# A hybrid attention and retention step on one core: an operand refilled block by block by a job, loads and trips moved, constant products in the opening

## The chip, the cores and the metric

The kernel runs on one core of a Trainium2 chip. A core has five engines that work from queues of their own: TensorE (PE in the profile; its weight loads are shown as PEld), VectorE (DVE), ScalarE (ACT), GpSimd (POOL) and SyncE (SP). SP does no arithmetic here; it issues transfers, and so do ACT and POOL beside their work. The metric is the time of one execution on the device in microseconds. A forecast counts as "the same" within 0.3%.

## The reference

One layer of a streaming encoder. Its input is normalised (RMSNorm) and multiplied by one matrix of 2048 x 8192, in eight parts of 8 heads x 128: queries, keys, values and gates of a stick-breaking attention (sb) and of a retention (ret). Cut to what the change touches:

```python
def stick_breaking_block(q, k, v, q_start):
    z = einsum('bqhd,bkhd->bhqk', q, k) * HEAD_DIM ** -0.5
    log_keep = where(strict, log_sigmoid(-z), 0.0)
    later = cumsum(log_keep, axis=3, reverse=True) - log_keep
    a = where(strict, exp(log_sigmoid(z) + later), 0.0)
    return einsum('bhqk,bkhd->bqhd', a, v)

def retention_chunk(q, k, v, s, log_gamma):
    scores = einsum('bihd,bjhd->bhij', q, k) * intra          # intra: decay gamma^|i-j|
    o = einsum('bhij,bjhe->bihe', scores, v) + einsum('bihd,bhde->bihe', q, s) * decay_read
    s_new = s * gamma^n + einsum('bjhd,hj,bjhe->bhde', k, decay_write, v)
    return o, s_new
```

Every branch's output is normalised per head and multiplied by SiLU of its gate; both go through one output matrix of 2048 x 2048, a second RMSNorm and a residual sum. This is done for a prompt of 1024 frames (retention from a zero state) and for 8 running streams of 16 frames each, which have 1024 cached keys and values per head and a retention state per head (`state_ret`). All is float32.

## The kernel before

**Tiles and groups.** The 1024 prompt frames are tiles 0 to 7 of 128 frames, the 8 x 16 sample frames are tile 8 (SAMPLE). Two groups go through the projections one after the other: group 0 holds tiles 0 to 3 and the sample tile, group 1 tiles 4 to 7. The normalised input of a group lies in on-chip memory as the operand `mov`: 16 blocks of 128 features (KT), each split into a high part `mh` and a low part `ml`, four blocks to a tile (WQ). Group 1's normalised input waits in the scratch tensor `s_h` until group 0 has been projected.

**Products.** Each float32 product of a projection is made of three: high x high, high x low and low x high. `split` (L129, L130) makes the parts: ACT writes the high one, DVE the difference. Weights come in blocks `wr` of 256 KB by SP (`load_w`, L213), are split into `wh` and `wl`, and `products` (L227) uses them. `project_rows` (L286) does the same with tokens as rows (`wrn`, `accn`). Weight tiles have four buffers; the tag `mr`, through which blocks of an operand are loaded, has two.

**The opening.** `load_x` brings a tile of x, `mean_square` and `stats` make its scale, `turn` (L370, L372) turns it with 16 products against a diagonal matrix (`dg`) or the identity into `p0t`, which `split` writes into `mov`. The first projection's products are put between the tiles. `stage_rest` prepares group 1's input and stores it in `s_h`.

**Jobs and ticks.** All the work of the heads other than projections is written as generators. A `Job` is stepped by `tick()`, which `products` and `project_rows` call: a tick is one step of a projection (two products in group 0, one in group 1), and at most one job is stepped in a tick. `yield n` waits n ticks. `drain(job)` ticks until a job is done, without products in between. The constants D_... hold those waits, mostly as a pair for group 0 and group 1. `tied(ins)` tells the scheduler, in group 0 alone, to place an instruction no earlier than the product issued last. Within these bounds a scheduler sets the order on each engine; each engine then works its queue in order.

**Retention.** `ret_branch` sends the rotated keys out to memory and reads them back transposed by 32 x 32 squares (`turn_out` by ACT, then `turn_in`, four loads `ro<-s_rk` by SP, then a transposition on DVE): the key trip, D_TO and D_TI ticks long. Then `retention` (L745) loads the head's decay tile `dT` (L747, by SP) and makes four rounds, one per tile: `rs` = keys x queries (L752), `sc` = rs x dT on DVE (L754), `pa` = values x sc (L770) and state x queries (L775), `pS` = keys x values (L785), the new state `S` on DVE. `sample_retention` then loads four pairs of states `st` (L806, by SP), waits, and does the same for the streams (L810 to L836). The head's result makes such a trip too (`Out.finish`: `s_o`, then `ro` or `so`, `do`).

**Attention.** `attention()` of a head projects the queries (`col(0, h)`), drains the attention jobs of the head before, and starts `decode` (the sample streams against the cache: `kc`, `kcT`, `zc`, `vc`, `pd`), then projects the keys (`col(1, h)`) and starts `sb_branch`. In `stick_breaking`, each step makes the scores `z` of one tile, the sigmoids `kp` and `be`, a running product on DVE and the weights; these go to memory by POOL's queue (`turn_out`), come back (`turn_in`) and are transposed on DVE (L576) before the product with the values (`pa`, L616). D_TB ticks lie between the weights and their way out.

**From group 0 to group 1.** With group 0's last head, the gates of both branches are projected together (`project_pair`), weight block by weight block, so that a quarter of `mov` comes free after each pair of blocks. `load_moving` (L205) fills it with group 1's operand: four blocks are drawn ahead of each of the last three pairs, and the last four in the first `project_rows` of group 1.

```python
for k in range(KT):
    r = pool.tile([P, n], F32, name="mr", tag="mr", bufs=bufs)
    nc.sync.dma_start(r, src(k))
    split(hi[q][:, j, at : at + n], lo[q][:, j, at : at + n], r)
    yield D_MR
```

**The end.** `out_panel` and `out_project` multiply by the output matrix, panel by panel; `gpost` is loaded when the heads' memory is free.

Of the kernel before, what the change touches and what calls it, by code (L numbers as in the profile page):

```python
# [58 lines left out]
def tile_hybrid_step(  # L59
# [240 lines left out]
    with ExitStack() as s1:  # L300
# [47 lines left out]
        with tc.tile_pool(name="p0", bufs=2) as p0, tc.tile_pool(name="p0s", bufs=1) as p0s, tc.tile_pool(  # L348
# [16 lines left out]
            def turn(q, xt, scale=None):  # L365
# [34 lines left out]
            for i, t in enumerate(tiles):  # L400
                if i + 1 < len(tiles):
                    scales.append(stats(i + 1))
                cs = slice(i * P, (i + 1) * P)
                for q in range(KT // 4):
                    pt = turn(q, loaded[i], scales[i])
                    split(mov[0][q][:, :, cs], mov[1][q][:, :, cs], pt)
                if i == 1:
                    w4 = list(load_w(col(4, 0)))
                    loaded += [load_x(t) for t in tiles[3:]]
                    acc = acc_banks(g0)  # L410
                    for w in w4:
                        products(mov, acc[:1], g0["pieces"][:1], *w)
# [147 lines left out]
        def stick_breaking(g, h, out, q2, k2, rest):  # L560
# [3 lines left out]
            for step in range(len(todo) + lag):  # L564
# [179 lines left out]

        def retention(gi, g, h, out, rq, rk, rkn, rv):  # L745
            dT = op.tile([P, 2, P], F32, name="dT", tag="dT", bufs=1)
            tied(nc.sync.dma_start(dT, c_dt[:, h]))  # L747

            def scores(i, kind):
# [11 lines left out]
            sc = scores(0, 0)  # L761
            yield D_RET[phase[0]]
            for i in range(4):
                nxt = None
                if i < 3:
# [31 lines left out]
            if SAMPLE in g["tiles"]:  # L797
                yield from sample_retention(h, out, sc, rq, rkn, rv)

        def sample_retention(h, out, sc, rq, rkn, rv):  # L800
            i = 4

            sts = []
            for c in range(4):
                st = ip.tile([P, 2, P], F32, name="st", tag="st", bufs=4)
                tied(nc.sync.dma_start(st, state_ret[0, 2 * c : 2 * c + 2, h].rearrange("b d e -> d b e")))  # L806
                sts.append(st)
            yield 2 * D_RET[phase[0]]
            po = acc_tile()
# [29 lines left out]
        def ret_branch(gi, g, h, rq, rk, rv, rest):  # L839
# [9 lines left out]
            tied(nc.vector.transpose(rkn.rearrange("p k d -> p (k d)")[:, : nt * P], raw))  # L849
# [3 lines left out]
            nc.vector.tensor_scalar(rkn[:, :4, :], rkn[:, :4, :], dec[:, h, 1:2], None, ALU.mult)  # L853
            yield from retention(gi, g, h, out, rq, rk, rkn, rv)
            while "rg" not in rest:
# [33 lines left out]

        from_h = lambda k: s_h[:, k, :]  # L890
        from_y = lambda k: s_y[0][k][:, : 3 * P]
        ret_job = sb_job = sub = loads = after = None
        for gi, g in enumerate(GROUPS):
# [7 lines left out]
            for h in range(H):  # L901
# [70 lines left out]
                def gates():  # L972
# [235 lines left out]
```

## Time and profile before

| | |
|---|---|
| median of 3 runs | 2404.76 us (2398.75 to 2406.34) |
| the profiled execution | 2400.08 us, span 2398.4 us |
| granted TensorE clock, mean | 0.994 |
| PE busy | 2331.4 us, 97% of the span |
| DVE, ACT, POOL busy | 1257.5, 919.6, 643.0 us |
| moved by DMA | 418.68 MB, mean 175 GB/s |

Times are in microseconds from the span's start. A row of the timeline gives start, length, engine, line, operation, output <- inputs and, in brackets, how long the engine stood idle before it and what ended that. A row of the waits gives the engine and line that waited, what for, the sum, the number and the longest. "x32" counts records; a float32 product of 128 x 128 leaves two. A name stands for all buffers of a tile. PEclk is the share of the clock that TensorE was granted.

Group 0's heads run from about 100 to 1120 us, group 1's to about 1985, the output panels to the end.

### The profile page before, as it was taken

Reading aid. Unit: us, or ns where it says so; the run is one execution under the profiler, and the core shown is the slowest. Engines: PE = TensorE matmul, PEld = TensorE weight load, DVE = VectorE, ACT = ScalarE, POOL = GpSimd, SP = SyncE. Lnnn points to the kernel's source line nnn. Section 1 sums busy time; section 2 is a strip of 40 time slices with the busy share of each in tenths; the row PEclk is TensorE's granted clock in tenths of the full one; section 3 lists DMA queues with packets and bytes.
Section 4 is the critical chain, followed back from the end, with each engine's and each line's share of the span. In section 5 each row is a group of like instructions: output and inputs, shape, how many; then the busy total and the mean of one; then the engine's idle time right before and its main releaser. Section 6 shows DMA issues by size and latency. Waiting matters only on the chain.

```text
span 2398.4 us, 40493 instructions
## 1 busy us (share of the span) xinstructions
PE 2331.4 (97%) x14832; PEld 2093.7 (87%) x14832; DVE 1257.5 (52%) x2434; ACT 919.6 (38%) x1933; POOL 643.0 (27%) x1029
## 2 busy tenths in 40 slices
PE   7999999999999999998999999999999999999998
PEld 7998899999999999988878889889898887878787
DVE  7245545445554555445545554554554665564544
ACT  6323333333333333324433434343343454543343
POOL 3144353444344353443202112020221230000000
PEclk9999999999999999999999999999999999999999
DMA  7658879797889879798975565565565666765554
GB/s 244 164 131 209 162 169 196 169 203 166 184 179 194 184 167 194 176 198 198 200 191 151 139 157 149 133 157 146 142 160 139 157 177 181 231 207 176 191 182 132
DMA packets 674890, 418.68 MB, mean 175 GB/s; under 512 B 224513, under 2 KB 619777, under 8 KB 672257
## 3 DMA queue, kind: packets, MB, share of 16 engines
q1 hardware_dynamic: 524272, 285.99, 47.8%
q0 software_dynamic: 32256, 71.36, 13.6%
q10 hardware_dynamic: 118160, 58.74, 9.1%
q8 instruction: 116, 1.90, 0.4%
q14 instruction: 86, 0.70, 0.1%
HBM read 336.24 MB, written 79.69 MB: 173 GB/s over the span
## 4 chain that ended last, share of the span: by engine, by line
PE 87%; DVE 4%; DMA 4%; issue 2%; ACT 1%; POOL 1%; ACTq 0%; DVEq 0%; SPq 0%; POOLq 0%
PE acc L227 45%; PE accn L286 17%; PE a L1029 5%; PE a L1030 5%; PE a L1028 5%; PE pa L616 3%; PE z L586 2%; DMA wr<-w_in 1%; PE zc L659 1%; PE pd L726 1%; DMA mr<-s_h 1%; DVE wl L130 1%; PE pa L770 1%; DVE out L1090 1%; PE rs L752 1%
## 5 line engine op out<-in xcount | busy, mean ns | idle before, releaser
L227 PE MATMUL acc<-mh,wh 128*128 128x256 f32 (+2 forms) x2304 | 664.3, 341 | 6.4 <-ACT wh L129 6.0
L227 PE MATMUL acc<-ml,wh 128*128 128x384 f32 (+2 forms) x2304 | 663.0, 340 | 0.0
L130 DVE TENSOR_TENSOR wl<-wr,wh 128x512 fp32r<-128x512 f32 (+1 forms) x576 | 392.7, 688 | 515.5 <-ACT wh L129 508.3
L227 PE MATMUL acc<-mh,wl 128*128 128x256 f32 (+2 forms) x2304 | 658.9, 339 | 0.6 <-DVE wl L130 0.5
L129 ACT ACTIVATE wh<-wr 128x512 fp32r<-128x512 f32 (+1 forms) x576 | 356.9, 624 | 713.1 <-PE acc L227 243.4
L227 PEld LDWEIGHTS acc<-mh,wh 128*128 128x128 f32 x2304 | 420.2, 189 | 43.3 <-ACT wh L129 7.1
L227 PEld LDWEIGHTS acc<-mh,wl 128*128 128x128 f32 x2304 | 424.4, 189 | 31.4 <-issue 2.1
L227 PEld LDWEIGHTS acc<-ml,wh 128*128 128x128 f32 x2304 | 422.6, 189 | 33.2 <-issue 5.3
L643 POOL DMA_DIRECT2D kc<-cache_sb_k x512 | 332.4, 655 | 369.8 <-DVE kcT L681 207.5
L286 PE MATMUL accn<-whn,mh 128*128 128x256 f32 x1152 | 329.0, 287 | 0.9 <-ACT whn L129 0.8
L286 PE MATMUL accn<-wln,mh 128*128 128x256 f32 x1152 | 326.2, 283 | 0.7 <-DVE wln L130 0.7
L286 PE MATMUL accn<-whn,ml 128*128 128x256 f32 x1152 | 326.0, 283 | 0.0
L286 PEld LDWEIGHTS accn<-whn,mh 128*128 128x128 f32 x1152 | 220.5, 192 | 10.8 <-issue 6.7
L1029 PE MATMUL a<-wl,mh 128*128 128x512 f32 (+1 forms) x576 | 219.7, 381 | 7.8 <-DVE wl L130 7.8
L286 PEld LDWEIGHTS accn<-wln,mh 128*128 128x128 f32 x1152 | 221.2, 192 | 1.7 <-DVE wln L130 0.9
L286 PEld LDWEIGHTS accn<-whn,ml 128*128 128x128 f32 x1152 | 221.2, 192 | 0.0
L1030 PE MATMUL a<-wh,ml 128*128 128x512 f32 (+1 forms) x576 | 218.9, 380 | 0.0
L1028 PE MATMUL a<-wh,mh 128*128 128x512 f32 (+1 forms) x576 | 218.0, 380 | 0.0
L130 DVE TENSOR_TENSOR wln<-wrn,whn 128x512 fp32r<-128x512 f32 x128 | 87.5, 687 | 119.2 <-ACT whn L129 118.5
L129 ACT ACTIVATE whn<-wrn 128x512 fp32r<-128x512 f32 x128 | 80.1, 633 | 152.2 <-PE accn L286 69.8
L1029 PEld LDWEIGHTS a<-wl,mh 128*128 128x128 f32 x576 | 108.3, 188 | 30.5 <-DVE wl L130 9.9
L479 POOL DMA_DIRECT2D be<-s_be x128 | 94.2, 742 | 132.7 <-DMA s_be<-be 114.7
(189 smaller groups left out, 2604.8 us busy)
## 6 DMA issues: line engine op xcount, KB each, us to landing
wr<-w_in SPq DMA_DIRECT2D x384, 256.0 KB, 4.2
wr<-w_out SPq DMA_DIRECT2D x184, 256.0 KB, 3.6
wrn<-w_in SPq DMA_DIRECT2D x128, 256.0 KB, 3.1
kc<-cache_sb_k POOLq DMA_DIRECT2D x512, 64.0 KB, 4.5
vc<-cache_sb_v SPq DMA_DIRECT2D x64, 512.0 KB, 8.6
xt<-x_prompt SPq DMA_DIRECT2D x8, 1024.0 KB, 5.6
xr<-x_prompt SPq DMA_DIRECT2D x8, 1024.0 KB, 6.2
out<-out ACTq DMA_DIRECT2D x12, 512.0 KB, 2.9
```

Of the source, the lines that this page charges most:

```text
L129: nc.scalar.activation(hi, src, AF.Copy)
L130: nc.vector.tensor_tensor(lo, src, hi.bitcast(F32), ALU.subtract)
L227: last = nc.tensor.matmul(a[:, :m], lhs[:, j, :], rhs[w][:, j, o : o + m], start=(w == 0 and j == 0 and n == 0), stop=(w == KT // WQ - 1 a ...
L286: anchor[0] = nc.tensor.matmul(a, lhs[q][:, jj, ts], rhs[:, j, :], start=(w == 0 and j == 0 and n == 0 and t % 2 == 0), stop=(w == KT // 2 ...
L479: q.dma_start(raw[32 * i : 32 * i + 32, :].rearrange("p (k a) -> p k a", a=32), s[:, :, 32 * i : 32 * i + 32].rearrange("k (j b) a -> b (k ...
L586: nc.tensor.matmul(z[:, :c], q2[a][:, i * P : (i + 1) * P], k2[b][:, s : s + c], start=(m == 0), stop=(m == 2),)
L616: nc.tensor.matmul(po[:, :P], at[:, j, :], vn[:, j, :], start=(j == 0), stop=(j == t))
L643: nc.gpsimd.dma_start(kc[32 * i : 32 * i + 32, :].rearrange("p (k d) -> p k d", d=32), cache_k[0, 2 * c + j, s * 512 : (s + 1) * 512, h, 3 ...
L659: mm = nc.tensor.matmul(z[r, :], qp[:, j, r], ready[2 * j + c // 2][:, c % 2, :], start=(j == 0), stop=(j == 1),)
L1028: nc.tensor.matmul(a[:, :width], hi[q][:, j, ts], wh, start=(k == 0), stop=False)
L1029: nc.tensor.matmul(a[:, :width], hi[q][:, j, ts], wl, start=False, stop=False)
L1030: nc.tensor.matmul(a[:, :width], lo[q][:, j, ts], wh, start=False, stop=(k == KT - 1))
```

## The change

1. In the opening, 32 products of a constant tile with itself (`busy`) are put before the first tile and 16 behind it. Their results are not read.
2. `dT` is loaded before the key trip's way back instead of after it, and the key trip has times of its own: D_RO = (32, 44) and D_RI = (32, 34) in place of (32, 23) and (32, 13).
3. The four `st` loads are issued at the third retention round instead of after the last, and the wait of 2 x D_RET ticks behind them goes.
4. D_TB of group 1 is 33 ticks instead of 24, and 22 in heads 4 to 6.
5. Group 1's operand is filled by a job of its own, `refill`: two blocks are loaded ahead; then every D_RF = 6 ticks one block is split and the next but one is loaded; loads and ACT's half of the split are tied to the products. Group 0 no longer draws from `load_moving`; group 1 does as before.

```diff
-D_TB = (17, 24)
+D_TB = (17, 33)
+D_TBL = 22
+WARM = (32, 16)
+D_RF = 6
+D_RO = (32, 44)
+D_RI = (32, 34)
...
+            busy = p0s.tile([P, P], F32, name="busy")
+            nc.vector.memset(busy, 1.37)
+
+            def busy_products(n):
+                pt = p0p.tile([P, 4, P], F32, name="p0t", tag="p0t")
+                for j in range(n):
+                    nc.tensor.matmul(pt[:, j % 4, :], busy, busy, start=True, stop=True)
+
             loaded = [load_x(tiles[0])]
+            busy_products(WARM[0])
...
+                if i == 0:
+                    busy_products(WARM[1])
...
-                        yield D_TB[phase[0]]
+                        yield D_TBL if H - 5 < h < H - 1 else D_TB[phase[0]]
...
-        def retention(gi, g, h, out, rq, rk, rkn, rv):
-            dT = op.tile([P, 2, P], F32, name="dT", tag="dT", bufs=1)
-            tied(nc.sync.dma_start(dT, c_dt[:, h]))
+        def retention(gi, g, h, out, rq, rk, rkn, rv, dT):
...
             for i in range(4):
+                if i == 2 and SAMPLE in g["tiles"]:
+                    for c in range(4):
+                        st = ip.tile([P, 2, P], F32, name="st", tag="st", bufs=4)
+                        tied(nc.sync.dma_start(st, state_ret[0, 2 * c : 2 * c + 2, h].rearrange("b d e -> d b e")))
+                        sts.append(st)
...
-            sts = []
-            for c in range(4):
-                st = ip.tile([P, 2, P], F32, name="st", tag="st", bufs=4)
-                tied(nc.sync.dma_start(st, state_ret[0, 2 * c : 2 * c + 2, h].rearrange("b d e -> d b e")))
-                sts.append(st)
-            yield 2 * D_RET[phase[0]]
...
-            yield D_TO[phase[0]]
+            dT = op.tile([P, 2, P], F32, name="dT", tag="dT", bufs=1)
+            tied(nc.sync.dma_start(dT, c_dt[:, h]))
+            yield D_RO[phase[0]]
             turn_in(s, raw, nc.sync)
-            yield D_TI[phase[0]]
+            yield D_RI[phase[0]]
...
+        def refill(mov):
+            hi, lo = mov
+            blocks = []
+
+            def load(k):
+                blocks.append(wp.tile([P, NB_TOK], F32, name="mr", tag="mr", bufs=2))
+                tied(nc.sync.dma_start(blocks[k], s_h[:, k, :]))
+
+            yield 2 * 3 * WQ - 2 * D_RF
+            load(0)
+            yield D_RF
+            load(1)
+            yield D_RF
+            for k in range(KT):
+                q, j = divmod(k, WQ)
...
+                tied(nc.scalar.activation(hi[q][:, j, :NB_TOK], blocks[k], AF.Copy))
+                nc.vector.tensor_tensor(
+                    lo[q][:, j, :NB_TOK], blocks[k], hi[q][:, j, :NB_TOK].bitcast(F32), ALU.subtract
+                )
+                if k + 2 < KT:
+                    load(k + 2)
+                yield D_RF
...
-                    loads = load_moving(after, 0, *((NB_TOK, from_h), (3 * P, from_y, (ip, 6)))[gi])
+                    if gi == 0:
+                        filling = Job(refill(after))
+                    else:
+                        loads = load_moving(after, 0, 3 * P, from_y, (ip, 6))
```

More of the change, by code (lines that the diff above doesn't have):

```diff
@@ L762, in retention @@
             yield D_RET[phase[0]]
+            sts = []
             for i in range(4):
+                if i == 2 and SAMPLE in g["tiles"]:
[3 more added lines that the diff above has]
+                        sts.append(st)
                 nxt = None
@@ L797, in retention, with sample_retention @@
             if SAMPLE in g["tiles"]:
-                yield from sample_retention(h, out, sc, rq, rkn, rv)
-        def sample_retention(h, out, sc, rq, rkn, rv):
+                yield from sample_retention(h, out, sc, rq, rkn, rv, sts)
+        def sample_retention(h, out, sc, rq, rkn, rv, sts):
             i = 4
-            sts = []
-            for c in range(4):
-                st = ip.tile([P, 2, P], F32, name="st", tag="st", bufs=4)
-                tied(nc.sync.dma_start(st, state_ret[0, 2 * c : 2 * c + 2, h].rearrange("b d e -> d b e")))
-                sts.append(st)
-            yield 2 * D_RET[phase[0]]
             po = acc_tile()
@@ L853, in ret_branch @@
             nc.vector.tensor_scalar(rkn[:, :4, :], rkn[:, :4, :], dec[:, h, 1:2], None, ALU.mult)
-            yield from retention(gi, g, h, out, rq, rk, rkn, rv)
+            yield from retention(gi, g, h, out, rq, rk, rkn, rv, dT)
             while "rg" not in rest:
```

3 lines of the change are left out of this document (added).

## The prediction

> **What bounds the kernel now.** I read the page's busy shares and chain first, then the stretches of 60 us, then every idle time of PE in its timeline.
>
> ```profile
> PE 2331.4 (97%) x14832; PEld 2093.7 (87%) x14832; DVE 1257.5 (52%) x2434; ACT 919.6 (38%) x1933; POOL 643.0 (27%) x1029
> PE 87%; DVE 4%; DMA 4%; issue 2%; ACT 1%; POOL 1%; ACTq 0%; DVEq 0%; SPq 0%; POOLq 0%
> ```
>
> TensorE is busy for 97% and carries 87% of the chain. The change takes no product of the reference away, so all it can win is PE's idle time, 2398.4 - 2331.4 = 67.0 us, and time at a lowered clock. Both sit in few places (columns: stretch, length, busy time of PE, PEld, DVE, ACT, POOL, granted clock, DMA share, GB/s):
>
> ```profile
> 0.00:60.00 60.00, 44.30 (x298) 43.20 (x299) 46.07 (x117) 38.81 (x64) 19.18 (x30) 0.97 0.74 244
> 240.00:300.00 60.00, 55.79 (x407) 52.65 (x406) 30.53 (x75) 19.16 (x45) 20.02 (x31) 0.94 0.82 163
> 1080.00:1140.00 60.00, 53.55 (x366) 48.36 (x364) 34.98 (x86) 27.07 (x62) 21.78 (x37) 0.97 0.80 196
> 1200.00:1260.00 60.00, 54.30 (x382) 47.03 (x381) 26.86 (x61) 21.09 (x46) 4.22 (x7) 0.94 0.71 192
> ```
>
> These four hold 15.7 + 4.2 + 6.5 + 5.7 us of idle PE. PE's timeline names the idle times in brackets, with what ended them:
>
> ```profile
> 10.63 6.71 PE L372 MATMUL p0t<-dg,xt 128*128 128x128 f32 x32 [10.63 <-DVE dg L389]
> 19.52 5.44 PE L372 MATMUL p0t<-dg,xt 128*128 128x128 f32 x32 [2.19 <-DVE p0v L137]
> 30.55 3.73 PE L372 MATMUL p0t<-dg,xt 128*128 128x128 f32 x32
> 270.88 0.80 PE L770 MATMUL pa<-rv,sc 128*128 128x128 f32 x2 [4.21 <-DVE sc L754]
> 541.77 0.49 PE L770 MATMUL pa<-rv,sc 128*128 128x128 f32 x2 [0.43 <-DVE sc L754]
> 543.68 0.56 PE L227 MATMUL acc<-mh,wl 128*128 128x256 f32 x2 [0.16 <-DVE wl L130]
> 1079.37 0.49 PE L770 MATMUL pa<-rv,sc 128*128 128x128 f32 x2 [0.43 <-DVE sc L754]
> 1114.06 0.90 PE L813 MATMUL pa<-st,rq 128*32 128x256 f32 x4 [2.33 <-DMA st<-state_ret]
> 1127.10 0.71 PE L830 MATMUL pSs<-rv,rkn 32*128 32x128 f32 x6 [2.27 <-DVE st L833]
> 1215.01 0.79 PE L227 MATMUL acc<-mh,wh 128*128 128x512 f32 x1 [5.40 <-ACT wh L129]
> 1298.28 1.83 PE L616 MATMUL pa<-vn,kp 128*128 128x128 f32 x14 [1.06 <-DVE kp L576]
> 1398.15 1.16 PE L616 MATMUL pa<-vn,kp 128*128 128x128 f32 x8 [0.66 <-DVE kp L576]
> ```
>
> An idle time also costs clock. Finer stretches:
>
> ```profile
> 20.50:23.50 3.00, 3.00 (x16) 3.00 (x16) 2.03 (x5) 1.81 (x4) 3.00 (x5) 0.50 1.00 384
> 30.00:40.00 10.00, 8.10 (x70) 7.74 (x69) 9.96 (x22) 6.87 (x14) 4.21 (x6) 1.00 0.58 182
> 266.70:276.00 9.30, 5.12 (x20) 4.84 (x21) 7.70 (x21) 3.59 (x9) 4.96 (x9) 0.64 1.09 217
> 1111.60:1124.00 12.40, 9.62 (x53) 7.27 (x52) 6.19 (x13) 4.21 (x10) 8.35 (x14) 0.86 1.05 238
> 1124.00:1147.00 23.00, 18.30 (x127) 15.42 (x126) 16.15 (x34) 12.29 (x23) 9.58 (x17) 0.93 0.71 178
> 1209.00:1219.00 10.00, 4.60 (x18) 3.69 (x17) 3.26 (x8) 2.92 (x8) 0.00 (x0) 0.66 0.84 226
> ```
>
> **The change, part by part.**
>
> *Opening (WARM).* 48 products of a constant are added: 32 (64 passes; the trace counts two for such a product) before tile 0, 16 (32 passes) between tiles 0 and 1. Nothing reads them. The rows at 10.63 and 30.55 show one tile at 6.71 and at 3.73 us, 0.21 and 0.117 us a pass; tile 1 takes 5.44. The cold price is 2.98 + 1.71 = 4.7 us, and 2.19 us of idle time lies between.
>
> ```profile
> 0.97 0.27 DVE L464 MEMSET par<- 128x256 f32 x1
> ```
>
> The constant's memset stands where this row is, so the products start near 1.2 us. Tile 0 took all its 6.7 us to come to speed, tile 1 some 3.5 (to 23.5). With 3.1 to 6.1 us at 0.23 us a pass, the 64 passes end at 10.4 to 11.8 us: against 10.63 nothing to 1.2 us late. Tile 0 then ends at 14.1 to 15.5 instead of 17.34, the second set at 17.9 to 19.3, tile 1 at 21.6 to 23.0 instead of 24.96: 1.9 to 3.3 us earlier. How much reaches the end of the opening is unknown: DVE is busy for 9.96 of the 10 us from 30 on, and only its earlier idle time can be won. Bounds: 1.2 us lost, 4.7 + 2.19 = 6.9 won. I take -2.5, near the middle of what tile 1 wins.
> The Trainium skill ("TensorE: Matmul & The Clock Gate", section on the HAM clock gate) says that the clock is released after about 3.4 us of sustained products, in a window that runs free. The 0.50 between 20.5 and 23.5 agrees. By its figure the first set would end at 1.2 + 3.4 + 49 x 0.117 = 10.3 us, and the sum would hold 0.3 us more gain, an estimate.
>
> *Decay tile and sample states in group 0.* The load of dT moves from after the key trip to before it; the four st loads move 36 ticks ahead of their first product instead of 18, and the 18 ticks of waiting go. Five issues per head are moved, past the ro trip (dT) or two retention rounds (st).
>
> ```profile
> 266.82 0.84 DVE L849 STREAM_TRANSPOSE rkn<-ro 128x640 f32<-128x640 f32 x1 [10.76 <-issue]
> 266.69 14.28 SPq L213 DMA_DIRECT2D wr<-w_in  x9
> 1109.31 1.96 SPq L806 DMA_DIRECT2D st<-state_ret  x4
> ```
>
> Head 1 (stall at 270.88): DVE stood still for 10.76 us until the key rows came, and the next weights were issued only at 266.69, so the wait for weights stays; but products of the retention, no longer behind dT, now fill it. Idle 4.2 us plus (1 - 0.64) x 9.3 = 3.3 us of clock, some 7 us in all, is the most that can go; nothing is the least. About ten products of 0.234 us (two passes at 0.117) done inside the wait save 2.3 us and part of the clock: -3.5.
>
> *The price of that.* In the built order of the changed kernel, heads 2 to 6 of group 0 have 22 products in a row (5 rs, 5 pa, 4 pS, 8 pd) between the query and the key projection of the attention, head 7 has 18, with no projection product among them. Before, dT stood behind them on SP's queue and the scheduler spread them over the next projection. The weights show why: before, one or two blocks of the key projection were loaded ahead of the so trip; now its first block is issued behind that trip. And on ACT its split stands behind the run's own squares and a table load.
>
> ```profile
> 531.86 17.20 SPq L213 DMA_DIRECT2D wr<-w_in  x9
> 536.02 0.38 PE L752 MATMUL rs<-rq,rk 128*128 128x128 f32 x2
> 537.71 0.63 ACT L129 ACTIVATE wh<-wr 128x512 fp32r<-128x512 f32 x1 [9.15 <-DMA wr<-w_in]
> 539.49 1.07 PE L726 MATMUL pd<-vc,kp 128*32 128x256 f32 x16
> 541.46 0.25 DVE L754 TENSOR_TENSOR sc<-rs,dT 128x128 f32<-128x128 f32 x1
> 543.23 1.14 ACT L129 ACTIVATE wh<-wr 128x512 fp32r<-128x512 f32 x2
> 544.56 0.62 ACT L129 ACTIVATE wh<-wr 128x512 fp32r<-128x512 f32 x1
> 545.19 1.28 ACT L138 ACT_TABLE_LOAD   x1
> ```
>
> PE's part of the run is 14 x 0.234 + 1.07 = 4.35 us. ACT: here the table load ends at 546.47, 4.7 us after the first pa; without the three splits ahead of it (1.8 us) 2.9, and with two rounds instead of one about 4.3 (an estimate: a round is six of these short steps of 0.2 to 0.3 us); a first pa comes 0.8 us into the run (rs, then sc at 0.25), the split takes 0.63 and a root 0.2 more: the first key product starts some 6.0 us into the run. PE idles 6.0 - 4.35 = 1.6 us, six times: +9.7. The stalls of 0.43 + 0.16 at 541.77 and 543.68, the first of three such heads (the last at 1079.37), go: -1.8. Together +8. The run begins where the first rs stands here, 536.02. A weight block issued at 531.86, 4.2 us ahead, landed by 537.71, 1.7 us into it: not the limit. Bounds per head: nothing (then -1.8 in all) and the 7 us of the stall at 270.88 (+42).
>
> *refill.* For the 16 blocks of group 1's operand, a job loads one block, splits it and loads the next but one, every 6 ticks; ACT's half is tied to the products. Before, four were drawn at a time, and ACT and SP queued behind them:
>
> ```profile
> ACT mh L129 <- DMA mr<-s_h: 17.5, 10, 5.0
> mr<-s_h SPq DMA_DIRECT2D x14, 256.0 KB, 4.1
> ```
>
> From 1111.6 to 1147 PE idles 2.78 + 4.70 = 7.5 us and loses (1 - 0.86) x 12.4 + (1 - 0.93) x 23 = 3.3 us of clock: 10.8 in all. The st wait (2.33 + 0.44) goes with its earlier load, and its clock loss of 1.7. What remains is bounded by the same two buffers: 4.1 us to land and two splits of 0.7 give 2.75 us a block, 44 us for 16, against 45 us in which they were split before; so ACT will still stand and wait, with weights behind it. I take half of the rest: -4.5 - 3 = -7.5, bounds -10.8 and 0.
> The Trainium skill (same page, "Architectural detail") calls the queues of ScalarE and VectorE strict FIFO, which speaks against tying a split to the products: wh waits behind an mh whose block is late. The 17.5 us above show it; were nothing won beyond the st wait, the sum would hold 3 us less.
>
> *Group 1's times.* D_TB goes from 24 to 33 ticks (22 in heads 4 to 6), the key trip from 23 + 13 to 44 + 34.
>
> ```profile
> PE pa L616 <- DVE kp L576: 5.0, 6, 1.1
> 1805.55 17.27 PE acc L227 x76
> ```
>
> A tick of group 1 is one product, 17.27 / 76 = 0.227 us; nine are 2 us, more than any of these six waits. Four fall in heads 0 to 3, twice 1.06 and 0.66 as at 1298.28 and 1398.15, 3.4 us in all, and go; two in heads 4 and 5 grow by 2 ticks, 0.45 us each. -2.5; bounds -5.0 (all go) and +2 (0.25 us a head, should the later key trip be felt). The retention job grows by 42 ticks and ends some 5 us later, while the first output panel runs; gpost is issued about 20 products later, and DVE's take as well, so the stall behind it keeps its size.
>
> *The wait at 1215.01* keeps its cause (weights behind two trips in the same order): 0, bounds -3 and +3.
>
> Sum: -2.5 - 3.5 + 8 - 7.5 - 2.5 = -8.0 us. The profiled execution took 2400.08 us (span 2398.4 and 1.7 around it), which gives 2392; the median of the runs is 4.7 us above it, 2404.76, and on that I forecast 2396.8, 0.33% less.
>
> **The rivals.**
> *The runs starve (slower).* If in heads 2 to 7 the block issued behind the trip lands late, each run ends in a wait like that at 270.88, with its clock. At 4 + 3 us each that is +42 - 1.8 against -16: 2429. It breaks even at 3 us a head and is slower by 0.3% from 4.2. For it: DMA is near full there, and the landing of a weight took 5.8 us at 537.71. Against it: the issue is 4.2 us ahead, and the run itself covers 4.35.
> *The runs cost nothing (faster).* If ACT's part is done inside the run, -16 - 1.8: 2387. For it: the even heads show no idle time there now; against it: the table load.
> *refill does not relieve.* Two buffers and the same landing leave the waits of 1124 to 1147 and add waits of wh: 2400 to 2404.
>
> **How the numbers follow.** As summed 0.50, alone 2388 to 2405; runs free 0.20, 2378 to 2390; runs starve 0.16, 2412 to 2429; no relief 0.14. 0.3% is 7.2 us, about what a measurement of this kernel can tell from no change. Faster: 0.34 of the first, 0.20, 0.04 of the last, 0.58; same 0.14 + 0.08 = 0.22; slower 0.02 + 0.16 + 0.02 = 0.20. The range 2377 to 2418 leaves out the ends of starving and half a tenth on the fast side.
>
> **What would show it.** Right: p0t at 3.7 us for tile 0 and tile 1; no st wait near 1114; no idle time of 4 us near 270; a gap of 1 to 2 us ahead of the key projection's first wh product in heads 2 to 7; fewer kp waits after 1290. Wrong: those gaps above 3 us or with a clock below 1, new waits of accn for whn near 1125, or a p0t start past 12 us.

## The result and the profile after

The changed kernel takes 2439.03 us (median, 2432.22 to 2441.29), the kernel before beside it 2405.55: a ratio of 1.0134, 95% interval 1.0099 to 1.017. It is 33.5 us slower. The profiled execution has a span of 2438.1 us, 39.7 more than the one of before.

Busy times of the changed kernel, from its page:

```profile
PE 2366.7 (97%) x14928; PEld 2118.9 (87%) x14928; DVE 1263.3 (52%) x2435; ACT 902.6 (37%) x1919; POOL 646.9 (27%) x1029
```

PE's idle time is 2438.1 - 2366.7 = 71.4 us, against 67.0: only 4.4 of the 39.7 us stand there. Busy time grew by 35.3 us, and only some 14 of them are the constant products. So the page hides most of the loss: short waits between dependent products, and products at a lower clock, count as busy. Both kernels run the same 10368 projection products in the same order, so I compared their traces by the start of the k-th of them, the changed kernel's minus that of before:

| projection products | place | lost there, us |
|---|---|---|
| 0 to 960 | opening, head 0 | 0.3 |
| 960 to 1632 | head 1 | 1.8 |
| 1632 to 6432 | group 0's heads 2 to 7 | 31.5 |
| 6432 to 7008 | from group 0 to group 1 | 7.6 |
| 7008 to 10176 | group 1's heads | -5.5 |
| 10176 to 10367 | last projections | -4.5 |
| 10367 to the end | output panels | 8.6 |

Two stretches of the changed kernel in the windows view (columns as in the prediction):

```profile
240.00:300.00 60.00, 55.13 (x392) 50.91 (x391) 27.29 (x70) 16.76 (x41) 18.64 (x29) 0.91 0.81 161
1200.00:1260.00 60.00, 49.78 (x255) 35.83 (x254) 28.21 (x57) 18.59 (x37) 3.68 (x8) 0.86 0.72 175
```

Both have less busy time than before (55.79 and 54.30) and a lower clock, but where the 31.5 us went this view doesn't show: that part is 822 us long, with PE busy for 98% of it. PE's timeline at head 4, from the first product of the run to the first query product behind it:

```profile
684.10 0.60 PE L766 MATMUL rs<-rq,rk 128*128 128x128 f32 x4
...
688.71 0.49 PE L790 MATMUL pa<-rv,sc 128*128 128x128 f32 x2 [0.28 <-DVE ro L799]
...
690.02 0.49 PE L805 MATMUL pS<-rv,rkn 128*128 128x128 f32 x2 [0.16 <-DVE S L810]
691.18 0.56 PE L232 MATMUL acc<-mh,wh 128*128 128x256 f32 x2 [0.67 <-ACT wh L134]
```

The brackets add up to 1.1 us, but the run of 22 retention and decode products takes 691.18 - 684.10 = 7.08 us. Spread over the projection the same 22 cost 4.35. This price is measured in g1_only, a kernel below that spreads them, as the delay of the projection until it is back at its pace: a single rs, pa or pS costs 0.22, a row of rs, pa and pa 0.68, the eight pd (sixteen records) 1.20, and the run holds eight singles and two such rows: 8 x 0.22 + 2 x 0.68 + 1.20 = 4.35 (from unrounded values). So 2.7 us are lost here, and 1.6 of them stand in no bracket.

ACT's timeline in the same place, from its last split before it:

```profile
671.52 0.63 ACT L134 ACTIVATE wh<-wr 128x512 fp32r<-128x512 f32 x1 [7.10 <-DMA wr<-w_in]
...
686.05 0.31 ACT L553 ACTIVATE sq<-ro 128x128 f32<-128x128 f32 x1 [9.40 <-DVE ro L793]
...
688.23 0.31 ACT L553 ACTIVATE sq<-do 128x128 f32<-128x128 f32 x1
...
689.11 1.28 ACT L143 ACT_TABLE_LOAD   x1
690.40 0.20 ACT L143 ACTIVATE or<-ov 128x1 f32<-128x1 f32 x1
690.51 0.61 ACT L134 ACTIVATE wh<-wr 128x512 fp32r<-128x512 f32 x1
```

The split that PE waits for is issued behind squares of ro and do, a table load and a root. Its weight block had landed at 686.32, by the trace's semaphores: 2.2 us after the run began and 4.2 us before the split. And SP's queue, first before, then after:

```profile
647.02 5.28 SPq L213 DMA_DIRECT2D wr<-w_in  x2
...
656.27 2.95 SPq L213 DMA_DIRECT2D wr<-w_in  x1
659.28 6.15 SPq L479 DMA_DIRECT2D ro<-s_rk  x4
665.54 3.49 SPq L479 DMA_DIRECT2D so<-s_o  x4
669.07 0.91 SPq L747 DMA_DIRECT2D dT<-c_dt  x1
670.08 2.78 SPq L213 DMA_DIRECT2D wr<-w_in  x4
```

```profile
661.31 2.12 SPq L859 DMA_DIRECT2D dT<-c_dt  x1
663.52 0.40 SPq L218 DMA_DIRECT2D wr<-w_in  x1
...
671.25 6.58 SPq L496 DMA_DIRECT2D ro<-s_rk  x4
677.93 2.35 SPq L496 DMA_DIRECT2D so<-s_o  x4
680.33 1.60 SPq L218 DMA_DIRECT2D wr<-w_in  x2
```

Before, three weight blocks stand between the load of be and the two trips (ro, so); after, dT stands there with one. The block that the product behind the run waits for is issued at 680.33, behind both.

### The profile page after: what moved, and what is told of

Read it like the earlier page. It is cut to its first block, busy times and chain, and to the rows that moved or that the text cites. A ratio compares the mean times of both kernels' runs of the same rounds, so it can differ in the third digit from the quotient of the medians.

```text
span 2438.1 us, 40624 instructions
## 1 busy us (share of the span) xinstructions
PE 2366.7 (97%) x14928; PEld 2118.9 (87%) x14928; DVE 1263.3 (52%) x2435; ACT 902.6 (37%) x1919; POOL 646.9 (27%) x1029
## 4 chain that ended last, share of the span: by engine, by line
PE 80%; DMA 9%; DVE 4%; issue 3%; ACT 2%; POOL 1%; SPq 1%; ACTq 0%; DVEq 0%; POOLq 0%
PE acc L232 42%; PE accn L291 16%; PE a L1075 4%; PE a L1076 4%; PE a L1074 4%; DMA kc<-cache_sb_k 3%; PE pa L633 3%; DMA mr<-s_y 2%; PE z L603 2%; PE pd L743 1%; PE zc L676 1%; DMA mr<-s_h 1%; DMA wr<-w_in 1%; DVE out L1136 1%; DVE ml L135 1%
## 5 line engine op out<-in xcount | busy, mean ns | idle before, releaser
L232 PE MATMUL acc<-ml,wh 128*128 128x256 f32 (+2 forms) x2304 | 660.9, 340 | 0.6 <-DVE p0u L147 0.6
```

What stands on the lines that cost most here:

```text
L232: last = nc.tensor.matmul(a[:, :m], lhs[:, j, :], rhs[w][:, j, o : o + m], start=(w == 0 and j == 0 and n == 0), stop=(w == KT // WQ - 1 a ...
```

## The experiments

The loss is read at two places of each head: at the boundary, where the run stands, and between the boundaries. The measure is the kernel g1_only, whose order on PE is that of before until group 1 (its own execution stood 1.3 us shorter at head 1's stall). A boundary is some 340 projection products long, from the start of the projection that holds the run; that of head 7 reaches into the change of groups. Sums over heads 1 to 7 at the boundaries and over heads 1 to 6 between them, in us more than g1_only:

| kernel | median us | ratio to before (95%) | boundaries | between |
|---|---|---|---|---|
| the change | 2439.03 | 1.0134 (1.0099-1.017) | 30.3 | 9.9 |
| dt_late | 2418.54 | 1.0064 (1.0041-1.0086) | 13.6 | 5.8 |
| st_late | 2412.42 | 1.0038 (1.0026-1.0051) | 6.1 | 6.2 |
| both_late | 2402.62 | 1.0002 (0.9989-1.0016) | -0.8 | 1.3 |
| wait_back | 2416.76 | 1.0054 (1.0039-1.0069) | 8.1 | 7.1 |
| early_states | 2402.37 | 0.9993 (0.9981-1.0006) | -0.5 | -0.3 |
| tied_rounds | 2450.77 | 1.0192 (1.0179-1.0206) | 46.3 | -0.2 |
| tied_squares | 2423.36 | 1.0080 (1.0065-1.0095) | 18.8 | 3.9 |
| tied_both | 2434.62 | 1.0128 (1.0107-1.0149) | 28.9 | 1.4 |
| dt_on_act | 2412.99 | 1.0035 (1.0021-1.0049) | 6.7 | 2.6 |
| dt_behind_trip | 2415.38 | 1.0045 (1.0029-1.0062) | 12.6 | 1.8 |
| trip_50 | 2396.88 | 0.9973 (0.9963-0.9983) | -8.2 | 0.0 |
| before_50 | 2452.25 | 1.0195 (1.0180-1.0210) | 18.8 | 27.7 |

**Which part.** dt_late: dT back behind the trip.

```diff
-            dT = op.tile(...); tied(nc.sync.dma_start(dT, c_dt[:, h]))    # in ret_branch, before D_RO
+            dT = op.tile(...); tied(nc.sync.dma_start(dT, c_dt[:, h]))    # in retention, first
```

> The changed kernel with one part undone: dT is again loaded after the key trip, inside the retention, in both groups. In its built order none of the runs of 22 products between query and key projection is left; the sample states are still loaded early. Theory A (the runs cost group 0 its time: products that depend on each other through DVE stand in a row, and the key projection's first split stands behind them): the loss of group 0, +35 us between the 960th and the 6432nd projection product, falls to within 5 us of zero, and the kernel takes 2400 to 2412 us. Theory B (the earlier loads of dT and st crowd the transfer queues, whatever the order of the products): at most half of the 35 us goes, 2420 us or more. Theory C (neither; the refill and the opening shifted the whole plan): no change, about 2439.

st_late: the four `st` loads back in `sample_retention`, with `yield 2 * D_RET[phase[0]]` behind them.

> The changed kernel with the other part undone: the four state loads are again issued after the last retention round, with the wait of 36 ticks behind them; dT stays early. The built order has a run of retention products with no projection product among them at two head boundaries (heads 1 and 6) in place of seven. Theory A: group 0 loses 3 to 4 us at each of these two and 1 to 2 us of a decode wait behind each, 8 to 12 us in place of 35: 2412 to 2418 us, and the trace shows it at those two boundaries alone. Theory B: dT's load is five times as early as before in all heads, so the loss is in all of them, 15 us or more: above 2420.

both_late: both of these.

> The changed kernel with both moves of loads undone: what is left is the opening's constant products, the refill job and group 1's times. No runs in the built order. Theory A and B alike: group 0 is as before to within 2 us; the rest shows alone: the opening -1.4, group 1's heads -5.5 as the two traces show them, and the stretch from group 0 to group 1, which in the changed kernel lost 8 us, tells whether refill or the early states cost it: near 0 if the states do, +5 or more if refill does. 2395 to 2410 us.

g1_only: before, with D_TB = (17, 33), D_TBL = 22, D_RO = (32, 44), D_RI = (32, 34).

> The kernel before with group 1's times alone changed (33 and 22 ticks ahead of the weights' way out, 44 and 34 for the key trip). If the 5.5 us that the changed kernel wins between the 7008th and the last projection product come from these times, they appear here too, and so do the 4 us that it loses in the output panels, if those come from the later retention of the last head: 2397 to 2405 us. If group 1's gain is only time returned that the stretch before it had lost, nothing is won here: 2405 or more.

With both moves undone group 0 is as before, so the two moves hold the whole loss there. With only one of them left the loss is 19.4 us (dt_late, 13.6 + 5.8) or 12.3 (st_late), with both 40.2. Neither of the two first theories holds: that the run is the price (A) missed in dt_late, which has no run and still loses 19; that the moved loads' traffic is (B) missed in st_late, which loses less than B's 15 us, and none at heads 3 and 5 (-0.2 each).

**The loads or the wait.** wait_back puts back one line, the wait; early_states has the wait back and dT late.

```diff
         def sample_retention(h, out, sc, rq, rkn, rv, sts):
             i = 4
+            yield 2 * D_RET[phase[0]]
```

> The changed kernel with one line added: the wait of 36 ticks (2 x 18) stands again between the four retention rounds and the streams' part. The state loads stay early, dT stays early. Its built order has the runs at the same two head boundaries as the kernel with late states, not at seven. Theory A1 (the wait that was taken away, not the place of the loads, brings all jobs into step so that the runs form): the time is that of the kernel with late states, 2412 us +- 5, with the loss at the same two boundaries, 27 us under the changed kernel. Theory B (the early state loads crowd the transfers): at least 8 us above the kernel with late states, 2420 or more.

> The changed kernel with dT late and the wait of 36 ticks back; only the four state loads are still early, beside the opening, refill and group 1's times. Against the kernel with both moves undone (2402.6 us) it tells the worth of early state loads by themselves. The wait for st at the end of group 0 (2.33 + 0.44 us before) should be gone; the prediction gave 4.5 us for it and its clock. Theory A1: no loss in group 0, 2396 to 2402 us. Theory B: a loss in every head, 2407 us or more.

Early loads of the states cost nothing (early_states: no loss in group 0). With dT early, giving back the wait alone takes the changed kernel to 2416.8, near st_late: the wait that was taken away counted, not where the loads stood. It shifts all later steps of the jobs by a few products, and the scheduler then makes another order.

One part of the wait's price can be read at each of heads 1 to 6: in the change the first eight of the streams' pSs records go in two parts of four, which costs 0.83 us more a head, and in wait_back they stay together. dt_late and the kernels with tied products have them apart as well.

**Moving the rounds.** trip_50 changes one number of the changed kernel, D_RO = (50, 44); before_50 does it in the kernel before, whose dT is late.

> The changed kernel with one number changed: the key trip's first part lasts 50 ticks in group 0 instead of 32. Everything else stays, dT and st early and no wait behind the rounds; the retention rounds fall 18 ticks later, and no run is left in the built order. Theory A (the runs are the price): group 0 loses at most 6 us in place of 34, and the kernel takes 2402 to 2412 us. Theory B (the early loads) or the missing wait by itself: group 0 keeps the 15 to 20 us that the kernel with late dT lost: 2416 us or more.

> The kernel before with one number changed: 50 ticks instead of 32 for the first part of the key trip in group 0. If the later rounds alone bring the 8 us that the kernel with 50 ticks won in group 0, they appear here: 2394 to 2399 us. If they need the early dT: within 3 us of before, 2401 to 2406.

trip_50 is faster than before: 2396.9 us, 0.9973. In its order the result's trip goes ahead of the key trip and four weight blocks ahead of both, and group 0 wins 8 us, most of it at heads 1 and 7; I had expected 2402 us or more. Head 1's stall in its timeline:

```profile
271.84 0.49 PE L790 MATMUL pa<-rv,sc 128*128 128x128 f32 x2 [0.48 <-DVE sc L768]
```

before_50 loses 47 us with the same number, where I had expected at most 2406: there PE waits for sc and sc for a late dT (2.4 to 2.9 us at heads 2, 3 and 4), and kb waits of up to 5.3 us follow. So with late rounds the early dT is worth having. The two kernels differ in more than dT, so how much of the 55 us between them is dT's is not shown.

**What holds the projection.** tied_rounds ties the rounds' first product to the projection, so that the run can't form:

```diff
-                nc.tensor.matmul(ps[:, :P], rk[:, bs], rq[:, bs], start=True, stop=True)
+                tied(nc.tensor.matmul(ps[:, :P], rk[:, bs], rq[:, bs], start=True, stop=True))
```

> The changed kernel with the product rs of each retention round tied to the projection product issued last, as the loads are. All numbers and loads stay (dT early, states early, no wait, key trip 32); the scheduler may no longer pull the rounds ahead of the key projection. In the built order the runs of 18 to 22 products are gone (one rs, one pa and eight pd are left there), while the decode's second bundle (zc) stays where the changed kernel has it, 12 products earlier than before. Theory A (the run is the price at the boundaries): of the 30 us lost at the seven boundaries at least 20 go. If the 10 us lost between the boundaries come from the place of the zc bundle, they stay: 2410 to 2418 us. If they follow from the runs, they go too: 2400 to 2408. Theory B (early loads crowd the queues): 2425 us or more.

Theory A fell here: without the run the kernel is 12 us slower still. Theory B's number holds, its mechanism is tested below (dt_on_act). PE's timeline of tied_rounds at head 4, then ACT's:

```profile
689.06 0.38 PE L766 MATMUL rs<-rq,rk 128*128 128x128 f32 x2
...
690.77 0.63 PE L743 MATMUL pd<-vc,kp 128*32 128x256 f32 x6
695.58 0.90 PE L232 MATMUL acc<-mh,wh 128*128 128x256 f32 x2 [4.18 <-ACT wh L134]
```

```profile
691.20 0.31 ACT L553 ACTIVATE sq<-ro 128x128 f32<-128x128 f32 x1 [9.60 <-DMA wr<-w_in]
...
693.09 0.31 ACT L553 ACTIVATE sq<-do 128x128 f32<-128x128 f32 x1 [1.49 <-DVE do L752]
...
693.51 1.28 ACT L143 ACT_TABLE_LOAD   x1
694.81 0.20 ACT L143 ACTIVATE or<-ov 128x1 f32<-128x1 f32 x1
694.92 1.65 ACT L134 ACTIVATE wh<-wr 128x512 fp32r<-128x512 f32 x3
```

The projection starts again 6.5 us after the first rs, against 7.1 with the run. So the run stands in a hole that PE would otherwise idle through. The Trainium skill ("TensorE: Matmul & The Clock Gate", section "Architectural detail") calls ACT's queue strict FIFO; that agrees with this view, where a split waits behind squares that wait for DVE (1.49 us), with PE standing still.

tied_squares ties the squares instead, so that ACT takes the split first; tied_both ties both.

```diff
-                nc.scalar.activation(sq, self.o[:, i, :], AF.Square, accum_out=self.ssq[:, i : i + 1])
+                tied(nc.scalar.activation(sq, self.o[:, i, :], AF.Square, accum_out=self.ssq[:, i : i + 1]))
```

> The changed kernel with the square of each finished row (sq, on ACT) tied to the projection product issued last. In the built order ACT now splits the query projection's third weight block ahead of the squares and the table load; the run of products on PE stays (it even holds two products more). Theory D (what sets the restart of the projection is ACT's queue: the split stands behind two squares, the table load and the root, whatever PE does meanwhile): the restart comes earlier by about the 2 to 3 us that these take, as far as the run lets it; the run itself needs 6.4 us, so it saves 0.7 us a head at least, 4 us or more in group 0: 2428 to 2436 us. Theory A (the run on PE alone is the price): no change, or 1 us more for the two products: 2438 to 2442.

> Both ties: rounds and squares. No run on PE, and ACT splits the third weight block first. The kernel with tied rounds alone stood still for 4.2 us at each head and took 2450.8 us. Theory D: the restart comes when the weights have landed and are split, some 2.5 us after the last product of the second block, 1.3 us of it filled: the loss at the boundaries falls from 46 to 5 to 15 us, and the kernel takes 2408 to 2420 us. Theory E (the weights themselves land late, ACT's order is not what holds them): the standstill stays, 2440 us or more.

tied_squares wins more than theory D said (2423.4 us): 1.0 us at each of heads 2 to 6 and 6.0 at head 7, where PE's wait behind the run falls from 1.71 to 0.89 us and no lowered clock follows. At head 4 no wait for weights is left in its timeline:

```profile
685.50 0.49 PE L790 MATMUL pa<-rv,sc 128*128 128x128 f32 x2 [0.31 <-DVE ro L799]
...
686.19 0.54 PE L232 MATMUL acc<-mh,wh 128*128 128x256 f32 x2
```

There the run's own chain of dependent products, 24 in 6.77 us, sets the restart. tied_both: ACT's timeline, then PE's, at head 4:

```profile
687.50 0.63 ACT L134 ACTIVATE wh<-wr 128x512 fp32r<-128x512 f32 x1 [9.33 <-DMA wr<-w_in]
688.66 0.63 ACT L134 ACTIVATE wh<-wr 128x512 fp32r<-128x512 f32 x1 [0.54 <-DMA wr<-w_in]
...
692.36 0.63 ACT L134 ACTIVATE wh<-wr 128x512 fp32r<-128x512 f32 x1 [1.45 <-DMA wr<-w_in]
```

```profile
685.62 0.38 PE L766 MATMUL rs<-rq,rk 128*128 128x128 f32 x2
...
688.18 0.56 PE L232 MATMUL acc<-mh,wh 128*128 128x256 f32 x2 [0.21 <-ACT wh L134]
```

Now ACT waits for each block to land, and the restart comes 2.56 us after the first rs: so early do these transfers allow it. The four kernels at head 4, with the products that fill the time at their spread price:

| kernel | first rs to restart | filled | difference | loss at head 4 |
|---|---|---|---|---|
| the change | 7.08 | 4.35 | 2.73 | 3.85 |
| tied_rounds | 6.52 | 1.65 | 4.87 | 7.26 |
| tied_squares | 6.77 | 4.80 | 1.97 | 2.77 |
| tied_both | 2.56 | 1.65 | 0.91 | 3.19 |

Of what the last column has more, 0.83 in each row are the streams' products in two parts. The rest is clock in tied_rounds (0.62 from 695.5 to 700) and further waits for weights in tied_both, where 18 records of the projection took 4.22 us instead of 2.73; in the change it is 0.3 behind the run. So without the run ACT's order costs 17.4 us over the seven boundaries (46.3 to 28.9), and the late weights most of what is left; with the run it costs 11.5 (30.3 to 18.8), and what is left at head 4 is the run's own chain and the streams. The sizes of theory D (late weights, with ACT's order on top) missed for tied_both (2408 to 2420 expected, 2434.6 measured): the late weights weigh more than I gave them.

**Why the weights are late.** dt_on_act issues dT from ACT's queue, dt_behind_trip on SP between the two trips.

```diff
-            tied(nc.sync.dma_start(dT, c_dt[:, h]))
+            tied(nc.scalar.dma_start(dT, c_dt[:, h]))
```

> The changed kernel with one word changed: dT is issued at the same place, but by ACT's queue instead of SP's. In the built order SP now has two weight blocks ahead of the two trips (ro, so) again, as before the change; in the changed kernel dT stood there with one block. The runs are left at heads 1 and 2 alone. Theory F (dT's place on SP pushed one weight block behind both trips, and everything at the boundaries follows from that): heads 3 to 7 lose at most 1 us each, group 0 at most 15 us, all of it in heads 1 and 2: 2402 to 2416 us. Theory B (dT's early transfer itself, or the missing wait): heads 3 to 7 keep 2 us or more each: 2420 us or more.

> The changed kernel with dT issued on SP behind the key trip's four loads, ahead of the result's trip (so). SP has two weight blocks ahead of both trips; runs at head 1 alone. Theory F: heads 2 to 7 lose at most 1 us each; 2400 to 2412 us, and less than the kernel with dT late (2418.5), because sc no longer waits for dT behind the second trip. If the kernel with late dT lost its 2 us a head to the missing wait and not to dT behind the second trip, this one loses them too: 2416 to 2420.

dt_on_act loses -0.2, 0.9, -0.2, 0.9 and -4.3 us at the boundaries of heads 3 to 7, in place of 2.7 to 6.2; what is left stands at heads 1 and 2, where its order still has runs. SP's queue can be counted: how many weight blocks fewer than before have been issued, from the kernel's start, when the key trip of heads 2 to 6 begins, and what those boundaries lose:

| kernel | blocks fewer | lost, us |
|---|---|---|
| the change | 2, 1, 2, 1, 2 | 3.8, 2.7, 3.9, 2.8, 3.8 |
| tied_rounds | 2, 1, 2, 1, 2 | 7.2, 7.3, 7.3, 7.3, 7.3 |
| dt_on_act | 2, 0, 1, 0, 1 | 3.8, -0.2, 0.9, -0.2, 0.9 |
| dt_behind_trip | 1, 0, 1, 0, 1 | 2.1, 1.3, 2.1, 0.9, 2.0 |
| dt_late | 1, 0, 1, 0, 1 | 2.3, 1.1, 2.3, 1.1, 2.3 |

Heads 3 and 5 read 1.1 us lower than 4 and 6 in most rows, because g1_only itself has the stall for sc there. In dt_on_act PE waits for no weights at heads 3 to 6; the 0.9 of heads 4 and 6 are the streams' 0.83. So, by this table and with dT off SP, one block fewer costs nothing at even heads and two cost the whole loss (head 2); at odd heads one is enough (the change). That bears out theory F, that dT's place on SP pushes weight blocks behind the trips; theory B, that dT's early transfer itself costs 2 us a head, fell. dt_behind_trip and dt_late missed their numbers though their counts are nearly those of dt_on_act. Their traces show what dT on SP still costs at head 4: in dt_behind_trip PE waits 0.92 us for a split of weights, in dt_late 0.71 for sc. At head 1 the count is the same in all of these kernels and in the one before, and 4.5 to 7.5 us are lost there all the same; the count does not explain those.

**The other parts.** refill_only is the kernel before with the job alone; tb_only has D_TB and D_TBL alone; trip_50_g0 is trip_50 with group 1's key trip at 23 and 13.

> The kernel before with the refill job alone. The prediction gave it 7.5 us, 4.5 of them by the st wait, which this kernel keeps; so 3 us by the prediction's step: 2400 us. The rival that two buffers and the same landing leave nothing to win: 2403 us +- 2, with the same 16 waits of mh for mr summing to 15 us or more.

> The kernel before with D_TB of group 1 alone changed (33; 22 in heads 4 to 6). The six waits for kp, 5.0 us, should go as the prediction said, without the 4.5 us lost at group 1's first head and the 7 us in the panels, if the later key trip brought those: 2399 to 2401 us. If those come with D_TB: 2403.

> The kernel with 50 ticks in group 0 (2396.9 us), with group 1's key trip set back to 23 + 13 ticks; D_TB stays 33 and 22. In that kernel 7.5 us were lost at group 1's first head and 8.2 us in the output panels, and 10 us won between. If the later key trip costs the first and the last of these: 2388 to 2393 us. If it also brings the gain between (the waits for kp gone): about 2397, no change.

refill_only takes 2400.3 us, 0.9986 (0.9975 to 0.9997). ACT still waits for mr, a little more than the 17.5 us of before (row of its waits):

```profile
ACT mh L922 <- DMA mr<-s_h: 19.7, 12, 2.8
```

tb_only is 2404.35 (0.9999, 0.9988 to 1.0010), g1_only 2403.13 (1.0002), trip_50_g0 2400.76 (0.9976, 0.9966 to 0.9986): group 1's times win nothing on either ground. The last projection product starts 6.3 us earlier in g1_only than before, and the end comes 0.9 us later. Heads' products behind it, groups by line, before and then g1_only (its two largest):

```profile
L616 PE MATMUL pa<-vn,kp 128*128 128x128 f32 x30 | 3.7, 277 | 0.0
```

```profile
L628 PE MATMUL pa<-vn,kp 128*128 128x128 f32 x42 | 5.2, 275 | 0.0
L787 PE MATMUL pa<-S,rq 128*128 128x128 f32 x8 | 1.5, 275 | 0.0
```

With 18 more of pS, pa and rs that makes 38 records, or 19 products: at 0.22 us each, some 4.2 us (an estimate) were only carried behind the mark. A panel's wait that the last section describes is longer too, 4.75 us here against 1.60 + 1.18.

## Why the prediction was wrong

I forecast 2396.8 us and gave "slower" 0.20; the kernel takes 2439.0. Point by point:

- *Opening, -2.5.* Its mechanism is right: tile 0 takes 3.74 us and tile 1 3.81 (rows below), and no time is lost at dg. The gain can't be told from chance: with the constant products the 288th projection product starts 1.0 to 1.6 us earlier than before, and in three of the four other kernels without them 1.4 to 1.7 earlier too, and in the fourth 0.1. PE's timeline:

```profile
1.16 9.98 PE L387 MATMUL p0t<-busy 128*128 128x128 f32 x64 [1.16 <-DVE busy L382]
10.98 3.74 PE L377 MATMUL p0t<-dg,xt 128*128 128x128 f32 x32
19.15 3.81 PE L377 MATMUL p0t<-dg,xt 128*128 128x128 f32 x32 [0.86 <-DVE p0v L142]
```

- *Head 1, -3.5.* Wrong in sign: +3.4 between the 1344th and the 1632nd product. The wait for sc gave way to three others, at a clock of 0.61 from 267 to 278 us:

```profile
268.27 0.49 PE L805 MATMUL pS<-rv,rkn 128*128 128x128 f32 x2 [2.71 <-DVE rkn L868]
270.24 0.80 PE L795 MATMUL pa<-S,rq 128*128 128x128 f32 x2 [0.86 <-DVE S L808]
275.64 0.80 PE L790 MATMUL pa<-rv,sc 128*128 128x128 f32 x2 [1.29 <-DVE ro L799]
```

- *The price of the moved loads, +8.* This is the step that failed: 31.5 us in heads 2 to 7. The mechanism was named (the block behind the trip, ACT's split behind squares and table load), its place was not: the run stands inside the query projection, behind its second weight block, not between query and key (in head 7 inside the key projection). The restart was mis-sized: it came 7.1 us after the first rs, not 6.0, and with 0.3 us behind it a run of heads 2 to 6 costs 3.0 us more than its products spread, not 1.6. What I took off for these products, 4.35, is what they cost elsewhere. "A weight block landed 1.7 us into it: not the limit" was read from the kernel before; in the changed one a block fewer or two stand ahead of the trips. Three terms were not in the sum at all. Without the wait the streams' products go in two parts: 0.83 us a head. At head 7 the run ends in an idle time of 1.71 us, with a clock of 0.51 from 1109.5 to 1116:

```profile
1109.77 0.90 PE L232 MATMUL acc<-mh,wh 128*128 128x256 f32 x2 [1.71 <-ACT wh L134]
```

Against this, the stalls of three heads went as forecast, 1.1 us each instead of the 0.6 that I took off. And 1 to 2 us a head are lost between the boundaries, by waits of the decode's zc for kcT, such as the one below; they go when the run goes (tied_rounds: -0.2). How they follow from the run I did not settle.

```profile
773.10 1.04 PE L676 MATMUL zc<-kcT,qp 128*32 128x512 f32 x2 [1.27 <-DVE kcT L698]
```

- *"The runs starve"*, the rival with 0.16, gave 2429 and broke even at 3 us a head. Measured are 31.5 / 6 = 5.2 a head, so its size was nearer than that of my sum. Its clock loss came at head 7 alone: in the runs of heads 2 to 6 no idle time is longer than 0.7 us, and the granted clock from 540 to 555 us is 1.00. It came at every head in tied_rounds, where the hole is not filled.
- *refill, -7.5.* Alone it wins 3.3 us, the "half of the rest" of the sum. The st wait of 2.33 us is gone in the changed kernel, but early states won nothing by it (early_states against both_late: 0.25 us by medians). In the changed kernel accn waits 7.5 us near the place where I had named a wait of accn for whn as a sign against, but it waits for rg, the gate that empties its accumulator, and ACT's stores of keys and states and the refill's mh stand ahead of the gates; PE's timeline, then ACT's:

```profile
1164.81 0.58 PE L291 MATMUL accn<-whn,mh 128*128 128x256 f32 x1 [7.50 <-DVE rg L318]
```

```profile
1154.25 0.34 ACTq L882 DMA_DIRECT2D out<-kn  x1
...
1160.48 0.93 ACTq L849 DMA_DIRECT2D out<-st  x2
1161.46 1.15 ACT L927 ACTIVATE mh<-mr 128x512 fp32r<-128x512 f32 x2 [8.20 <-DMA out<-kn]
```

- *Group 1's times, -2.5.* Five of the six kp waits go, as said; 19 products move behind the last projection, a delay of the job that I had put at 5 us without a price, and a panel waits longer (below). Nothing is left.
- *The wait at 1215, 0.* The wait of 5.40 us gave way to several, of which the longest is shown; the stretch from the 6720th to the 7008th product loses 8.7 us, in g1_only 4.3. The longest, of zc for kcT, comes with the refill job: it is 2.46 us in refill_only and 0.17 in g1_only. The others, four of 1.3 to 1.8 us for vc, do and rkn after 1245, come with group 1's later key trip: g1_only has such waits, while refill_only, tb_only and trip_50_g0, with the old key trip there, keep a wait for wh (2.6 to 6.1 us).

```profile
1205.83 1.92 PE L676 MATMUL zc<-kcT,qp 128*32 128x512 f32 x2 [3.60 <-DVE kcT L698]
```

## What to carry to other kernels

When a load is moved ahead on a queue that also brings weights, count how many weight blocks stand ahead of the next slow transfers before and after; here one or two blocks fewer at each head went with most of a loss of 30 us, and issuing the same load from another queue gave 26 us of the kernel's time back. A run of small products in a built order can be a filling as well as a cause: ask what the products behind it wait for, and price it by the time of the restart less what the filling would cost elsewhere, measured until the main work is back at its pace. Compare two traces by the start of the k-th product of the main work, since busy shares hide both dependent products and time that only moved past the end.

## What the runs showed of the hardware

An idle time of 4.18 us lowered the granted clock to 0.62 for the next 4.5 us (tied_rounds), one of 7.5 us to 0.59 for 8 us (the change, from 1164). Idle times up to 0.7 us in the runs of heads 2 to 6, and the one of 1.27 us at 773.10, left it at 1.00. Between them it varies: 1.71 us at head 7 lowered it to 0.51 for 6.5 us, 1.73 us in tied_both (at 1102.44) did not, 1.00 over the next 6.6. And DVE's last product of a panel slows when POOL works on rows of the same panel. Groups by line around the panel, before and then after:

```profile
L1090 DVE SCALAR_TENSOR_TENSOR out<-out,out3r,xr 128x1024 f32<-128x1024 f32 x4 | 7.0, 1816 | 0.0
```

```profile
L1136 DVE SCALAR_TENSOR_TENSOR out<-out,out3r,xr 128x1024 f32<-128x1024 f32 x4 | 9.1, 2336 | 0.0
L1134 POOL TENSOR_TENSOR out<-out,xr 128x1024 f32<-128x1024 f32 x2 | 6.8, 3403 | 127.7 <-ACT out L1133 127.7
```

Before, one of POOL's two products runs beside DVE's four; after, both do: 2336 ns instead of 1816, and the weights' split behind them makes PE wait 4.70 us, where before there were two waits of 1.60 and 1.18. The mean hides two sizes: in both traces a DVE product takes 1.27 to 1.29 us, or 3.36 to 3.43 when a POOL product is under way as it starts and has 2.3 us or more to go; at this panel there is one of the long ones before and there are two after, and each ends 1.1 us after POOL's product. It comes with D_TB: tb_only has the two long ones, refill_only has one. The Trainium skill ("GPSIMD Engine Reference", section "Specifications") says that GpSimd shares its SBUF interfaces with VectorE and contends with instructions of two SBUF inputs; these rows agree.
